# A two-layer hybrid trunk: three small moves in the order of VectorE, ScalarE and the load queue

## The chip, the cores and the metric

The kernel runs on one core of one Trainium2 chip. The metric is the device time of one execution in microseconds: 747.57 us before the change, the median of 3 runs (747.02 to 748.11).

## What is computed

256 tokens of width 1024 go through two layers in float32. Each layer has a token mixer and a gated ConvFFN, each behind an RMSNorm whose scale, shift and gate come from a conditioning vector c (adaLN). Layer 0 mixes by three dilated attention groups with 16 heads, layer 1 by gated linear attention (GLA) with 4 heads in chunks of 64 tokens.

```python
for i in range(2):
    mod = silu(c) @ w_ada[i] + b_ada[i]            # shift, scale, gate; twice
    h = rmsnorm(x, norm_mix[i]) * (1 + sc1) + sh1
    y = dilated_mixture(h, ...) if i == 0 else gla_mixer(h, ...)
    x = x + g1 * y
    h = rmsnorm(x, norm_ffn[i]) * (1 + sc2) + sh2
    x = x + g2 * conv_ffn(h, ...)
return rmsnorm(x, norm_final)

# gla_mixer, per head and chunk
gk = log_sigmoid(glr @ w_gate + b_gate) / 16
bcum = cumsum(gk);  blast = bcum at the chunk's end
q_t, k_t, k_d = q * exp(bcum), k * exp(-bcum), k * exp(blast - bcum)
A = tril(q_t @ k_t.T);  o = A @ v + q_t @ state
```

## The kernel before

**Weights.** Every product keeps float32 accuracy by splitting both factors into a high and a low part. A weight tile goes through four steps: SP's queue loads it into one of 4 `raw` buffers, ScalarE casts the high part `whi` (L236; L484 in the first pass), VectorE subtracts it for the low part `wlo` (L240; L582), and TensorE makes three products of each pair of blocks (L255 to L257): hi x hi, lo x hi, hi x lo. `whi` and `wlo` have 3 buffers each. SP's queue issues its loads in order, and a load waits there until its buffer is free.

**Order.** The order of instructions on each engine comes from a timeline simulation when the program is built; `behind(...)` is the only means by which the source bends it. It says that an instruction is to be placed behind another in that order and adds no wait by itself.

**The first pass (about 14 to 48 us)** computes q, k and v of head pairs 0 and 1, one k-tile (`kt` = 0 to 7) after another. For each kt, SP loads 2 x 512 KB of adaLN weights and a weight tile of 1920 columns (`load_w`, L589 to L595): 768 columns that the first 6 blocks need (`FRONT`) and 1152 more (`REST`). VectorE makes the dot products of the adaLN weights with c (L179), ScalarE turns each into the scale or shift (`mod`, L190 and L192) and makes `hhi` (L558), VectorE `hlo` (L574). TensorE's products of a front are L521.

**The pairs (about 50 to 262 us).** For pair u = 2 to 7 there are three groups g of queries and keys. Each has one weight tile `wqk` (1 MB). After each group's products `evacuate` takes q and k out of PSUM: for g = 0 in high and low parts (ScalarE L841, L842, VectorE `q` L845 twice and `k` L847), for g = 1 and 2 plainly (`k` L835). Ahead of group 2's products stand the 12 transposes (L798, `turn_all`) of the probabilities `pn` (VectorE L762, L763) of the pair before. At group 2, the first product takes its inputs from copies (`level`, shown as `q`) that share their buffer with a pair's q. Then come two tiles `wv` of 1536 columns for the values, whose subtractions are 128x768 twice each, then the scores and the softmax. Between them VectorE takes adaLN dot products of later sub-layers (`next_half`, 512 KB each, three spare buffers, loads at L691, dots at L179): three behind group 1 and three behind group 2.

**The gates (about 485 to 502 us).** `gates_of` (L1340) runs twice: for head 0, and for heads 1 to 3 together (tiles of 768 columns). It makes the decay sums `cs` by a scan (L1359), `u` = cs less its value at the chunk's end (L1362), and from these `e_q`, `e_k` and `e_d` by exponentials on ScalarE. `scaled_head` (L1449) multiplies q and k by them into `q_t`, `k_t`, `k_d`; `masked_head` makes the products L1475 of them. `head(n)` splits the q and k weights of head n, two subtractions of 128x1024.

Of the kernel before, what the change touches and what calls it, by code (L numbers as in the profile page):

```python
# [16 lines left out]
ALU = mybir.AluOpType  # L17

P = 128
# [9 lines left out]
CH = 64  # L29
# [30 lines left out]
def trunk(ctx: ExitStack, tc: tile.TileContext, I, out):  # L60
    nc = tc.nc
# [18 lines left out]
    @contextmanager  # L80
    def behind(*those):

        with ExitStack() as st:
            for i in those:
                st.enter_context(tc.issue_after(i.ins))
            yield
# [65 lines left out]
    for n in range(2):  # L152
        c = slice(512 * n, 512 * n + 512)
# [68 lines left out]

    last_load, copied, last_lo, dotted = [None], [None], [None], [None]

    def split(src, n, dmas=1, after=((), ()), late=(), low=(), view=None):
        raw = wraw.tile([P, 2048], F32, tag="raw", name="raw")
        for i in range(dmas):
            c = slice(n * i // dmas, n * (i + 1) // dmas)
            last_load[0] = nc.sync.dma_start(raw[:, c], src[:, c])
        hi = wspl.tile([P, 2048], F32R, tag="whi", name="whi")  # L230
        lo = wspl.tile([P, 2048], F32R, tag="wlo", name="wlo")
        part = view or (lambda w: w)
        for i in range(0, n, n // 2):
            c = slice(i, i + n // 2)
            with behind(*after[i > 0]):
                copied[0] = nc.scalar.copy(part(hi[:, c]), part(raw[:, c]))  # L236
        for i in range(0, n, n // 2):
            c = slice(i, i + n // 2)
            with behind(*(late if i else low)):
                last_lo[0] = nc.vector.tensor_tensor(part(lo[:, c]), part(raw[:, c]), part(hi[:, c].bitcast(F32)), op=ALU.subtract)  # L240
        return hi, lo
# [230 lines left out]
    part = tmp.tile([P, T], F32, tag="sqacc", name="part")  # L472
# [22 lines left out]
    for i, (g, n) in enumerate(ROWS):  # L495
        for first in range(0, n, P):
            c = slice(at, at + P)
# [90 lines left out]

    def load_w(kt, *queue):  # L589
        raw = wholes[1] if kt == 2 else wraw.tile([P, 2048], F32, tag="raw", name="raw")  # L590
        for c in (slice(0, 6 * P), slice(6 * P, 15 * P)) if kt < 3 else (slice(0, 15 * P),):
            with behind(*queue):
                last_load[0] = nc.sync.dma_start(raw[:, c], I["w0"][kt][:, c])
            queue = last_load[:1]
        return raw  # L595
# [27 lines left out]
    done = front(0, ((0, 0),), range(2 * NG), last_row)  # L623
    done = front_values(0, ((0, 0),), done)
    done = front(0, ((1, 0), (0, 1)), range(2 * NG), done)
    done = front_values(0, ((1, 0),), done)
    done = back_terms(0, HIGH, done)
    done = front_values(0, ((0, 1),), done)
# [261 lines left out]
    for u in range(NPAIR):  # L890
# [15 lines left out]
        if u < 2:  # L906
            for g in range(NG):
                evacuate(q, k, g, (pqk, pqk1)[u][2 * g], (pqk, pqk1)[u][2 * g + 1], *first_values[1:])
        else:
            for g in range(NG):  # L910
                low = negated[-1:] if (u, g) == (2, 2) else ()
                w = split(I["wqk"][u - 2, g], 2048, after=(ready, ready) if (u, g) == (2, 2) else ((), ()), low=low, late=low)
                if (u, g) == (2, 2):
                    with behind(last_lo[0]):
                        for _ in range(4):
                            second_pair[2]()
                    for _ in range(2):
                        next_half(norms[-1], turned[1], done)
                if (u, g) == (2, 1):
                    with tc.issue_after(last_load[0].ins):  # L920
                        bias = load_bias(1)
                    with behind(last_lo[0]):
                        for _ in range(4):
                            before[2]()
                    with behind(done):
                        second_pair = scores(1, *held, bias, *mm_k)
                pqk = bank("pqk", "p")
                pq, pk = pqk[:, :T], pqk[:, T:]
                for kt in range(KT):
                    s, e = kt == 0, kt == KT - 1  # L930


                    hk = early_level if u == 2 and g < 2 and kt == 0 else level if (u, g) > (3, 1) and g != 1 and kt == 0 else h[kt]
                    with behind(*(last_t if (g, kt) == (2, 0) else last_s if u == 2 and kt == 0 else [])):
                        mm3(pq[:, :T], parts(w, 2 * P * kt), hk, s, False)
                    mm_k = [mm3(pk[:, :T], parts(w, 2 * P * kt + P), hk, False, e)]
                if g == 1:
                    turn_all(before, pt := new_pt(), *mm_k)
                if (u, g) == (NPAIR - 1, 2):
                    copy_level((o_hi[OLEVEL], o_lo[OLEVEL]), *turned[-2:-1])  # L940
                done = evacuate(q, k, g, pq, pk)
                if (u, g) == (2, 2):
                    turn_all(second_pair, second_pt := new_pt(), *mm_k)
                if (u, g) == (2, 0):
                    first_loads.append(last_load[0])
                if g == 0:
                    ready = evacuated[:1]
                if u > 2:
                    for _ in range((0, 3, 3)[g]):
                        next_half(done)  # L950
                if g == 2 - (u > 2):
                    second = list(evacuated)
            if u == 4:
                with behind(last_load[0]):
                    nc.sync.dma_start(x_all, I["xT"])
        if u > 0:
            pv = [bank("pv", "p") for _ in range(2)]
            for half in range(2):
                with behind(*chain[7]):


                    if half == 1 and u < 4:
                        hi, lo = (first_values[:1], ()) if u == 1 else (second[:1], second[1:])
                    elif u == 2:
                        hi, lo = exps[7:8], last_dot[:1]
                    else:
                        hi = lo = ()
                    w = split(I["wv"][u - 1, half], 1536, after=(hi, hi if u < 3 else ()), low=lo, late=(*lo, done) if u == 2 and half == 0 else lo if u == 2 else ())
                    if u == 2 and half == 1:
                        for _ in range(3):  # L970
                            next_half(last_lo[0])
                if u > 1 and half == 0:
                    with tc.issue_after(last_load[0].ins):
                        bias = load_bias(u)
                for k4 in range(4):
                    kt = 4 * half + k4
                    wv = parts(w, 384 * k4, 384)
                    for t in range(2):
                        ht = [y[:, P * t : P * t + P] for y in h[kt]]
                        with behind(*(last_t if u == 2 and kt == 0 else [])):  # L980
                            last_pv[:] = [mm3(pv[t][:, :384], ht, wv, kt == 0, kt == KT - 1)]
# [358 lines left out]
    def gates_of(first, n):  # L1340
        def new(name, tag, columns=n * T):
            return gt([P, columns], name, tag=f"{tag}{min(first, 1)}")
# [12 lines left out]
        with behind(*offsets):  # L1355
# [2 lines left out]
        cs = new("cs", "cs")  # L1358
        nc.vector.tensor_tensor_scan(cs, keep[:, : n * T], sp, 0.0, op0=ALU.mult, op1=ALU.add)  # L1359
        cs4 = cs.rearrange("p (n t c) -> p n t c", t=2, c=P)  # L1360
        u = new("u", "C")
        offsets.append(nc.vector.tensor_tensor(u.rearrange("p (n t c) -> p n t c", t=2, c=P), cs4,  # L1362
                                               cs4[:, :, :, CH - 1 : CH].to_broadcast([P, n, 2, P]), op=ALU.subtract))
        e_d, e_q, e_k = (new(name, t) for name, t in (("e_d", "D"), ("e_q", "A"), ("e_k", "B")))
        d4 = e_d.rearrange("p (n t c) -> p n t c", t=2, c=P)
        nc.scalar.activation(e_k, u, AF.Exp, scale=1.0 / 16)
# [42 lines left out]
    with behind(last):  # L1409
        last = log_gates()  # L1410
    pv.append([bank("pv", "t") for _ in range(2)])
    gates = [gates_of(*part) for part in PARTS]
    with behind(*low_rank):
        w = columns(2, 0)
        next_ada(last_lo[0])
# [11 lines left out]
    def head(hd, **kw):  # L1427
        y = heads[hd]
        if hd == 0:
            y["w"] = split(I["w_qk_b"][0][:, KT * P :], KT * P)  # L1430
            y["pq"], y["pk"] = early_q, bank("pqk", "p")[:, :T]
        else:
            y["w"] = split(I["w_qk_b"][hd], 2048, **kw)
            pqk = bank("pqk", "p")
            y["pq"], y["pk"] = pqk[:, :T], pqk[:, T:]
# [103 lines left out]
    scaled_head(0)  # L1539
    head(1)  # L1540
    last = project_head(1, range(KT))
    head(2, low=first_kt[:1], late=first_kt[:1])
    last = masked_head(0, last)
    level = {kt: [gt([P, T], "lv", F32R, tag=tg) for tg in tags] for kt, tags in ((0, ("A0", "B0")), (1, ("C0", "D0")))}
    with behind(*copies):
# [156 lines left out]
```

## Time and profile before

| | before |
|---|---|
| median of 3 runs | 747.57 us (747.02 to 748.11) |
| profiled execution | 750.7 us, span 748.9 us |
| TensorE (PE) busy | 738.4 us, 99% |
| VectorE (DVE) busy | 645.5 us, 86% |
| ScalarE (ACT) busy | 490.0 us, 65% |
| DMA | 187.20 MB, mean 250 GB/s |

By stages, each busy time in us:

| window | TensorE | VectorE | ScalarE | DMA |
|---|---|---|---|---|
| 14 to 48 (first pass) | 33.21 | 32.37 | 24.71 | 412 GB/s |
| 100 to 246 (pairs 3 to 7) | 143.69 | 128.77 | 88.98 | 287 GB/s |
| 486 to 504 (gates) | 17.62 | 16.55 | 13.30 | 259 GB/s |

A row of a timeline gives: start in us, duration in us, engine and line, operation, output<-inputs, shapes, how many (x2 means two in a row in one line, whose duration runs from the first's start to the last's end), and in square brackets how long the engine had been idle and what ended that. Durations of matmuls are modelled and overlap: the row of 128x256 products has 0.28 us each, while they start 0.11 to 0.12 us apart. SPq rows are the issue of a DMA, not its transfer.

### The profile page before, as it was taken

The page shows a single profiled execution, that of the slowest core. Times are in us where ns is not written, and L with a number is a line of the kernel's source. Part 1 is how long each engine was busy: PE and PEld are TensorE (multiplying, and loading weights), DVE is VectorE, ACT ScalarE, POOL GpSimd, SP SyncE. Part 2 cuts the span into 40 slices and gives each one's busy share as a digit, 9 for nine tenths or more (in the row PEclk, how much of TensorE's full clock was granted, in tenths as well). Part 3 has the DMA queues.
Part 4 walks back from the last instruction along what each step waited for, and adds up shares of the span by engine and source line. Part 5 has one row for each costly group of instructions (what it writes and reads, how often), then busy time and mean ns, then how long its engine had stood idle before and what let it go on. Part 6 is the DMA issues. An engine that isn't in the chain of part 4 may idle for free.

```text
span 748.9 us, 16025 instructions
## 1 busy us (share of the span) xinstructions
PE 738.4 (99%) x6371; PEld 723.3 (97%) x6371; DVE 645.5 (86%) x1196; ACT 490.0 (65%) x967; POOL 30.8 (4%) x60
## 2 busy tenths in 40 slices
PE   9999999999999999999999999999999999999997
PEld 7999999999999999999999999999999999999996
DVE  6998998889988869999999886898969999997592
ACT  7686766556556568766766555866768676666551
POOL 1001010101101010000000100000010000000100
PEclk9999999999999999999999999999999999999999
DMA  9997779788788338877645997766758766774621
GB/s 340 412 399 272 261 267 393 251 274 312 251 302 281 114 140 305 307 262 263 226 161 190 322 327 242 282 232 225 274 184 284 279 221 233 206 182 159 206 97 57
DMA packets 40779, 187.20 MB, mean 250 GB/s; under 512 B 9170, under 2 KB 11866, under 8 KB 28032
## 3 DMA queue, kind: packets, MB, share of 16 engines
q1 hardware_dynamic: 40320, 185.73, 70.9%
q8 instruction: 50, 0.82, 0.4%
q10 hardware_dynamic: 304, 0.34, 0.1%
q14 instruction: 25, 0.20, 0.1%
q0 software_dynamic: 80, 0.11, 0.0%
HBM read 185.06 MB, written 1.10 MB: 249 GB/s over the span
## 4 chain that ended last, share of the span: by engine, by line
PE 85%; DMA 7%; DVE 5%; ACT 1%; issue 1%; DVEq 0%; SPq 0%; ACTq 0%
PE pab L256 11%; PE pab L255 11%; PE pab L257 10%; PE pd L255 5%; PE pd L257 5%; PE pd L256 5%; PE pqk L255 5%; PE pqk L257 4%; PE pqk L256 4%; DMA raw<-in_w 3%; PE pv L256 2%; PE pv L257 2%; PE pv L255 2%; PE py L255 2%; PE py L256 2%; PE py L257 2%
## 5 line engine op out<-in xcount | busy, mean ns | idle before, releaser
L240 DVE TENSOR_TENSOR wlo<-raw,whi 128x1024 fp32r<-128x1024 f32 (+5 forms) x248 | 264.5, 1094 | 25.8 <-ACT whi L236 25.0
L236 ACT CAST whi<-raw 128x1024 fp32r<-128x1024 f32 (+5 forms) x248 | 222.6, 943 | 96.4 <-PE pab L256 55.0
L256 PE MATMUL pab<-hlo,whi 128*128 128x256 f32 x672 | 184.9, 277 | 0.0
L257 PE MATMUL pab<-hhi,wlo 128*128 128x256 f32 x672 | 184.9, 276 | 0.0
L255 PE MATMUL pab<-hhi,whi 128*128 128x256 f32 x672 | 182.9, 277 | 0.0
L256 PEld LDWEIGHTS pab<-hlo,whi 128*128 128x128 f32 x672 | 126.1, 188 | 0.5 <-DVE hlo L335 0.4
L257 PEld LDWEIGHTS pab<-hhi,wlo 128*128 128x128 f32 x672 | 126.2, 188 | 0.0
L255 PEld LDWEIGHTS pab<-hhi,whi 128*128 128x128 f32 x672 | 125.0, 188 | 0.4 <-ACT hhi L333 0.3
L179 DVE CUSTOM_DVE_ANT_0 ada_raw<-ada_raw,c_bc 128x1024 f32<-128x1024 f32 x82 | 97.5, 1222 | 12.3 <-DMA ada_raw<-in_w_ada 12.1
L255 PE MATMUL pqk<-hhi,whi 128*128 128x256 f32 x354 | 97.7, 278 | 0.0
L256 PE MATMUL pqk<-hlo,whi 128*128 128x256 f32 x354 | 97.3, 277 | 0.0
L257 PE MATMUL pqk<-hhi,wlo 128*128 128x256 f32 x354 | 96.0, 277 | 0.2 <-DVE wlo L240 0.2
L257 PE MATMUL pd<-ghi,wlo 128*128 128x256 f32 x308 | 84.9, 276 | 0.0
L256 PE MATMUL pd<-glo,whi 128*128 128x256 f32 x308 | 84.9, 276 | 0.0
L255 PE MATMUL pd<-ghi,whi 128*128 128x256 f32 x308 | 84.7, 276 | 0.0
L255 PEld LDWEIGHTS pqk<-hhi,whi 128*128 128x128 f32 x354 | 66.5, 188 | 0.1
L256 PEld LDWEIGHTS pqk<-hlo,whi 128*128 128x128 f32 x354 | 66.5, 188 | 0.0
L257 PEld LDWEIGHTS pqk<-hhi,wlo 128*128 128x128 f32 x354 | 65.6, 188 | 0.4 <-DVE wlo L240 0.4
L256 PEld LDWEIGHTS pd<-glo,whi 128*128 128x128 f32 x308 | 57.8, 188 | 0.0
L257 PEld LDWEIGHTS pd<-ghi,wlo 128*128 128x128 f32 x308 | 57.8, 188 | 0.0
L255 PEld LDWEIGHTS pd<-ghi,whi 128*128 128x128 f32 x308 | 57.7, 188 | 0.0
L256 PE MATMUL pv<-wlo,hhi 128*128 128x384 f32 (+2 forms) x160 | 52.9, 332 | 0.0
(321 smaller groups left out, 1494.5 us busy)
## 6 DMA issues: line engine op xcount, KB each, us to landing
raw<-in_w_up SPq DMA_DIRECT2D x42, 1024.0 KB, 5.0
ada_raw<-in_w_ada SPq DMA_DIRECT2D x22, 1024.0 KB, 5.2
raw<-in_w_down SPq DMA_DIRECT2D x28, 704.0 KB, 4.4
ada_raw<-in_w_ada SPq DMA_DIRECT2D x38, 512.0 KB, 6.2
raw<-in_wqk SPq DMA_DIRECT2D x18, 1024.0 KB, 6.8
raw<-in_wv SPq DMA_DIRECT2D x14, 768.0 KB, 6.8
raw<-in_w SPq DMA_DIRECT2D x5, 960.0 KB, 12.8
raw<-in_w_v_b SPq DMA_DIRECT2D x6, 768.0 KB, 5.1
```

Source lines behind the costliest of these rows:

```text
L179: i = dotted[0] = nc.vector.tensor_tensor_reduce(w, w, c_bc, op0=ALU.mult, op1=ALU.add, scale=1.0, scalar=0.0, accum_out=dot,)
L236: copied[0] = nc.scalar.copy(part(hi[:, c]), part(raw[:, c]))
L240: last_lo[0] = nc.vector.tensor_tensor(part(lo[:, c]), part(raw[:, c]), part(hi[:, c].bitcast(F32)), op=ALU.subtract)
L255: mm(ps, a[0], b[0], start=start, stop=False)
L256: mm(ps, a[0], b[1], start=False, stop=False)
L257: return mm(ps, a[1], b[0], start=False, stop=stop)
```

## The change

It has three parts; the orders of TensorE and GpSimd stay as they were.

1. **Values' weights in the pairs.** In pairs 3 to 7 the two subtractions for the first `wv` tile are placed behind `keys_done`, the low part of group 0's key (`done` of g = 0, the instruction of L847).
2. **First pass.** `load_w` loads the tiles of kt = 3 and 4 in two transfers as well (768 and 1152 columns), as for kt = 1 and 2.
3. **Gates.** `gates_of` is cut in two; the second half, `factors_of`, makes `u` and the exponentials. For heads 1 to 3 it is called from within head 2's `split`, between its two subtractions, by the new argument `between`, and the second subtraction is placed behind `u`.

```diff
-    def split(src, n, dmas=1, after=((), ()), late=(), low=(), view=None):
+    def split(src, n, dmas=1, after=((), ()), late=(), low=(), view=None, between=None):
...
             c = slice(i, i + n // 2)
+            if i and between:
+                late = between()
             with behind(*(late if i else low)):
                 last_lo[0] = nc.vector.tensor_tensor(part(lo[:, c]), part(raw[:, c]), part(hi[:, c].bitcast(F32)), op=ALU.subtract)
...
-        for c in (slice(0, 6 * P), slice(6 * P, 15 * P)) if kt < 3 else (slice(0, 15 * P),):
+        for c in (slice(0, 6 * P), slice(6 * P, 15 * P)) if kt < 5 else (slice(0, 15 * P),):
...
                 if g == 0:
-                    ready = evacuated[:1]
+                    ready, keys_done = evacuated[:1], done
...
                     else:
-                        hi = lo = ()
-                    w = split(I["wv"][u - 1, half], 1536, after=(hi, hi if u < 3 else ()), low=lo, late=(*lo, done) if u == 2 and half == 0 else lo if u == 2 else ())
+                        hi, lo = (), (keys_done,) if u > 2 and half == 0 else ()
+                    late = lo if u == 2 or half == 0 else ()
+                    if (u, half) == (2, 0):
+                        late = *lo, done
+                    w = split(I["wv"][u - 1, half], 1536, after=(hi, hi if u < 3 else ()), low=lo, late=late)
...
         cs4 = cs.rearrange("p (n t c) -> p n t c", t=2, c=P)
+        return new, cs4, n
+
+    def factors_of(new, cs4, n, *after):
         u = new("u", "C")
-        offsets.append(nc.vector.tensor_tensor(u.rearrange("p (n t c) -> p n t c", t=2, c=P), cs4,
-                                               cs4[:, :, :, CH - 1 : CH].to_broadcast([P, n, 2, P]), op=ALU.subtract))
+        with behind(*after):
+            offsets.append(nc.vector.tensor_tensor(u.rearrange("p (n t c) -> p n t c", t=2, c=P), cs4,
+                                                   cs4[:, :, :, CH - 1 : CH].to_broadcast([P, n, 2, P]), op=ALU.subtract))
         e_d, e_q, e_k = (new(name, t) for name, t in (("e_d", "D"), ("e_q", "A"), ("e_k", "B")))
...
-    gates = [gates_of(*part) for part in PARTS]
+    gates = [factors_of(*gates_of(*PARTS[0]))]
+    sums_1 = gates_of(*PARTS[1])
...
-    head(2, low=first_kt[:1], late=first_kt[:1])
+    def later_factors():
+        gates.append(factors_of(*sums_1, *last_lo))
+        return offsets[-1:]
+
+    head(2, low=first_kt[:1], between=later_factors)
```

What this makes of the order, at three places. Line numbers of the changed kernel are higher by 2 to 10 than those before.

VectorE in a pair from 3 on, at the end of the softmax of the pair before and behind group 0's products. Before:

```order
L762 TENSOR_SCALAR pn<-prob,m 128x256
L763 TENSOR_SCALAR pn<-prob,m 128x128
L240 TENSOR_TENSOR wlo<-raw,whi 128x768 x2
L845 SCALAR_TENSOR_TENSOR q<-pqk,q 64x256 x2
L847 TENSOR_TENSOR k<-pqk,k 128x256
L240 TENSOR_TENSOR wlo<-raw,whi 128x768
L802 COPY pt<-t 128x512
L835 COPY k<-pqk 128x256
```

and now:

```order
L764 TENSOR_SCALAR pn<-prob,m 128x256
L765 TENSOR_SCALAR pn<-prob,m 128x128
L847 SCALAR_TENSOR_TENSOR q<-pqk,q 64x256 x2
L849 TENSOR_TENSOR k<-pqk,k 128x256
L242 TENSOR_TENSOR wlo<-raw,whi 128x768 x3
L804 COPY pt<-t 128x512
L837 COPY k<-pqk 128x256
```

The two subtractions went behind q and k, and stand directly ahead of the third.

ScalarE in the first pass, from the last cast of kt = 4 to the last of kt = 5. Before:

```order
L484 CAST whi<-raw 128x768
L190 ACTIVATE mod<-dot,one_b,small 128x1
L484 CAST whi<-raw 128x768
L192 ACTIVATE mod<-dot,small 128x1
L558 ACTIVATE hhi<-early_x,mod 128x256
L558 ACTIVATE xr<-early_x,mod 128x256
L484 CAST whi<-raw 128x384
```

and now:

```order
L486 CAST whi<-raw 128x768
L190 ACTIVATE mod<-dot,one_b,small 128x1
L192 ACTIVATE mod<-dot,small 128x1
L486 CAST whi<-raw 128x768
L560 ACTIVATE hhi<-early_x,mod 128x256
L560 ACTIVATE xr<-early_x,mod 128x256
L486 CAST whi<-raw 128x384
```

The cast of kt = 5's front went behind the second `mod`; at kt = 3, 4, 6 and 7 the order stays cast, then `mod`.

VectorE in the gates, from the scan for heads 1 to 3 on. Before:

```order
L1359 SCALAR_TENSOR_TENSOR cs<-keep,sp 128x768
L1362 TENSOR_TENSOR u<-cs 128x768
L1369 TENSOR_TENSOR e_d<-cs 128x3x128
L1459 TENSOR_TENSOR k_t<-pqk,e_k 128x256
L1463 SCALAR_TENSOR_TENSOR q_t<-early_q,e_q 128x256
L1465 TENSOR_TENSOR k_d<-pqk,e_d 128x128
L240 TENSOR_TENSOR wlo<-raw,whi 128x1024 x2
L1459 TENSOR_TENSOR k_t<-pqk,e_k 128x256
```

and now:

```order
L1364 SCALAR_TENSOR_TENSOR cs<-keep,sp 128x768
L1378 TENSOR_TENSOR e_d<-cs 128x3x128
L1469 TENSOR_TENSOR k_t<-pqk,e_k 128x256
L1473 SCALAR_TENSOR_TENSOR q_t<-early_q,e_q 128x256
L1475 TENSOR_TENSOR k_d<-pqk,e_d 128x128
L242 TENSOR_TENSOR wlo<-raw,whi 128x1024
L1371 TENSOR_TENSOR u<-cs 128x768
L242 TENSOR_TENSOR wlo<-raw,whi 128x1024
L1469 TENSOR_TENSOR k_t<-pqk,e_k 128x256
```

`u` went from ahead of everything of head 0 to between head 2's subtractions. On ScalarE the exponentials `e_k` and `e_q` of heads 1 to 3 went with it, behind the two casts of head 3's weights; and head 0's masked copy (L1478) now stands ahead of head 3's subtractions instead of behind them.

## The prediction

> **What bounds the kernel now.** I read the page's first part, then TensorE's and VectorE's waits in the stretch of the head pairs (100 to 246 us), then the timelines of the engines around each place that the diff touches.
>
> ```profile
> span 748.9 us, 16025 instructions
> PE 738.4 (99%) x6371; PEld 723.3 (97%) x6371; DVE 645.5 (86%) x1196; ACT 490.0 (65%) x967; POOL 30.8 (4%) x60
> ```
>
> TensorE is busy 99%: it is the bound taken over the whole, and only its few stops can be won back. The waits of the pairs' stretch (line waited for: us in total, times, longest), TensorE's and below them VectorE's:
>
> ```profile
> PE pqk L255 <- DVE k L847: 2.3, 3, 0.8
> ```
> ```profile
> DVE ada_raw L179 <- DMA ada_raw<-in_w_ada: 7.2, 7, 2.2
> ```
>
> TensorE stops three times for VectorE, 2.3 us. But VectorE itself stops seven times for a DMA. So inside the pairs two loops run beside each other, and a gain on TensorE lasts only if VectorE's loop can follow. That is the choice on which part A hangs.
>
> **A, the pairs.** The place, in pair 4, on TensorE, VectorE, ScalarE and the SP queue (the order of TensorE's and GpSimd's instructions is the same before and after):
>
> ```profile
> 140.01 1.47 PE L798 MATMUL t<-ident,pn 128*128 128x128 f32 x12
> 142.21 0.36 PE L255 MATMUL pqk<-q,whi 128*128 128x256 f32 x1 [0.73 <-DVE k L847]
> ```
> ```profile
> 138.92 1.82 DVE L240 TENSOR_TENSOR wlo<-raw,whi 128x768 fp32r<-128x768 f32 x2
> 140.77 0.86 DVE L845 SCALAR_TENSOR_TENSOR q<-pqk,q 64x256 fp32r<-64x256 f32 x2
> 141.64 0.42 DVE L847 TENSOR_TENSOR k<-pqk,k 128x256 fp32r<-128x256 f32 x1
> 141.98 0.95 DVE L240 TENSOR_TENSOR wlo<-raw,whi 128x768 fp32r<-128x768 f32 x1
> ```
> ```profile
> 138.80 0.77 ACT L841 ACTIVATE q<-pqk 64x256 fp32r<-64x256 f32 x2
> 139.59 0.37 ACT L842 CAST k<-pqk 128x256 fp32r<-128x256 f32 x1
> ```
> ```profile
> 139.01 2.09 SPq L229 DMA_DIRECT2D raw<-in_wqk  x2
> 144.43 0.33 SPq L229 DMA_DIRECT2D raw<-in_wv  x1
> 145.90 2.62 SPq L691 DMA_DIRECT2D ada_raw<-in_w_ada  x3
> ```
>
> Two subtractions L240 (1.82 us) stand between pn and q, k; the change puts them behind k. Then q waits for ScalarE instead: its halves end near 139.2 and 139.6, k's cast at 139.59 + 0.37 = 139.96. So VectorE's q runs at 139.2 and 139.65, k at about 140.1 to 140.5. The twelve transposes end by about 141.4, after k: the stop of 0.73 goes, and with it about 0.09 of restart (that first matmul takes 0.36 where its neighbours take 0.28). Over three pairs that is 2.3 + 3 x 0.09 = 2.6 us, the upper bound; at the level of k alone, 1.6 us more than now is the most that one pair could carry to the next.
>
> What pays: VectorE has waited for ScalarE a little, so its third L240 starts near 142.2 instead of 141.98, +0.2 in pairs where ScalarE is that late, and I take 0.3 over all five (in three of them the DMA stops take part of it up). And what is behind them on VectorE:
>
> ```profile
> 144.65 1.22 DVE L179 CUSTOM_DVE_ANT_0 ada_raw<-ada_raw,c_bc 128x1024 f32<-128x1024 f32 x1
> ...
> 153.81 1.23 DVE L179 CUSTOM_DVE_ANT_0 ada_raw<-ada_raw,c_bc 128x1024 f32<-128x1024 f32 x1 [2.16 <-DMA ada_raw<-in_w_ada]
> ```
>
> The row at 144.65 frees a buffer when it ends (145.87); at 145.90 SP issues the next three loads; at 153.81 VectorE has waited 2.16 us for them. From there VectorE works to the next pair's pn with no stop that TensorE causes. Since VectorE waits in this loop for the load and not for TensorE, an earlier TensorE doesn't shorten it: it is at best unchanged, by my estimate 0.3 us later. TensorE meets it again at the end of the pairs, at the first transpose of the last pair's pn, ahead of which the last piece of pn is written:
>
> ```profile
> 256.70 0.49 PE L784 MATMUL t<-ident,pn 128*128 128x128 f32 x3
> ```
> ```profile
> 255.65 0.28 DVE L763 TENSOR_SCALAR pn<-prob,m 128x128 f32<-128x128 f32 x1
> ```
>
> 256.70 - (255.65 + 0.28) = 0.77 us is all that TensorE may come earlier there. So A gives 0.77 - 0.3 = about 0.45 us, and the rest turns into new waits at the transposes (L798 of later pairs, L784). Each pair's moved pair of L240 also frees a raw buffer 1.6 us later, and the second load of the pair's wqk (the second of the x2 row at 139.01, which ran behind that release at 140.75) is issued that much later. The first wqk load is still under way then, so I cost it at nothing; if that cover is gone, it is the slow rival below. Bounds of A: -2.8 to +2.6.
>
> **B, the first pass.** The first weight cast and the mod row behind it on ScalarE for tiles 3 and 5, the same places on VectorE and on TensorE, and the DMA engines' answer for 6 to 36 us:
>
> ```profile
> 28.15 0.84 ACT L484 CAST whi<-raw 128x768 fp32r<-128x768 f32 x1 [1.86 <-DMA raw<-in_w]
> 28.90 0.29 ACT L192 ACTIVATE mod<-dot,small 128x1 f32<-128x1 f32 x1
> ...
> 38.23 0.84 ACT L484 CAST whi<-raw 128x768 fp32r<-128x768 f32 x1 [1.40 <-DMA raw<-in_w]
> 38.98 0.29 ACT L192 ACTIVATE mod<-dot,small 128x1 f32<-128x1 f32 x1
> ```
> ```profile
> 28.27 0.09 DVE L179 DVE_READ_ACCUMULATOR2_ANT dot<- 128x1 f32 x1
> 29.02 0.96 DVE L582 TENSOR_TENSOR wlo<-raw,whi 128x768 fp32r<-128x768 f32 x1 [0.67 <-ACT whi L484]
> ...
> 39.10 0.96 DVE L582 TENSOR_TENSOR wlo<-raw,whi 128x768 fp32r<-128x768 f32 x1 [0.27 <-ACT whi L484]
> ...
> 41.12 0.42 DVE L574 TENSOR_TENSOR hlo<-xr,hhi 128x256 fp32r<-128x256 f32 x1
> ```
> ```profile
> 29.87 0.96 PE L521 MATMUL pqk<-hhi,whi 128*128 128x256 f32 x6 [0.62 <-ACT hhi L558]
> ...
> 31.52 0.95 PE L521 MATMUL pqk<-hlo,whi 128*128 128x256 f32 x6
> ...
> 41.91 0.84 PE L521 MATMUL pqk<-hlo,whi 128*128 128x256 f32 x6
> ```
> ```profile
> DMA packets 3039, 12.16 MB, mean 405 GB/s; under 512 B 361, under 2 KB 363, under 8 KB 3037
> ```
>
> The second piece of a split tile, 128 x 1152 x 4 bytes = 0.59 MB, is 1.46 us at 405 GB/s, so the first lands that much earlier: tile 3's cast could start at 26.7. Its mod row must then wait for the dot that ends at 28.36; hhi and TensorE follow 0.5 us earlier than now, and VectorE's chain behind it 0.66 earlier. At tile 5, which isn't split, the change has mod ahead of the cast on ScalarE. The dot before it moves from 38.84 to about 38.4 (VectorE's earlier chain meets an adaLN load), so mod ends at 38.7, the cast starts at 38.75 instead of 38.23, and VectorE's 39.10 becomes 39.6. So does its hlo: 41.12 + 0.42 + 0.5 = 42.05, where TensorE used it at 41.91. The 0.5 won at tile 3 is waited away at tile 5, and 0.15 to 0.2 more. B: -0.2. Bounds: if VectorE is not earlier at all, the cast starts at 39.2 and B is -0.6; if tile 5 does no harm, the gain at the hlo row, +0.7. Two more issues on SP (0.33 us each in the rows of this queue) lie in a queue that runs 12 us ahead. The Trainium skill, "DMA: Bandwidth & Descriptors", section Bandwidth, speaks against B: it wants transfers of at least 1 MiB for 75% of peak and gives 341 GB/s at 1 MB. An estimate by that page: a tile's 0.98 MB at 341 instead of 405 GB/s is 0.45 us later, twice, and B would be -1.1. The trace disagrees: the 405 GB/s here is a stream of pieces of 0.4 to 1 MB.
>
> **C, the gates.** TensorE and VectorE around the first masked head:
>
> ```profile
> 493.38 0.28 PE L257 MATMUL pqk<-hhi,wlo 128*128 128x256 f32 x1
> 493.88 0.49 PE L1475 MATMUL a<-q_t,k_t 128*128 128x128 f32 x2 [0.23 <-DVE q_t L1463]
> ...
> 495.22 0.39 PE L257 MATMUL pqk<-hhi,wlo 128*128 128x256 f32 x1 [0.16 <-DVE wlo L240]
> ```
> ```profile
> 491.74 0.96 DVE L1362 TENSOR_TENSOR u<-cs 128x768 f32<-128x768 f32 x1
> 492.61 0.55 DVE L1369 TENSOR_TENSOR e_d<-cs 128x384 f32<-128x384 f32 x1
> 493.08 0.42 DVE L1459 TENSOR_TENSOR k_t<-pqk,e_k 128x256 f32<-128x256 f32 x1
> 493.41 0.42 DVE L1463 SCALAR_TENSOR_TENSOR q_t<-early_q,e_q 128x256 f32<-128x256 f32 x1
> 493.75 0.28 DVE L1465 TENSOR_TENSOR k_d<-pqk,e_d 128x128 f32<-128x128 f32 x1
> 493.95 2.35 DVE L240 TENSOR_TENSOR wlo<-raw,whi 128x1024 fp32r<-128x1024 f32 x2
> ```
>
> u (0.87 us from its start to e_d's) leaves the place ahead of e_d, so q_t ends at 492.96 instead of 493.83 and the first wlo half at about 494.3 instead of 495.15. TensorE reaches the masked head at 493.5: the first stop, 0.50 between starts less a pace of 0.11, 0.39 us, goes. It then wants the wlo near 494.5: the second stop, 0.34 between the same kind of starts, and its 0.11 of restart go too. Sum 0.84; I take 0.8. Late next: u ends at 495.1 between the two halves, the second half at 496.2 for products that come near 497; ScalarE's e_k and e_q for the other heads move behind head 3's casts to 495.1 to 496.8, so q_t of head 1 is 0.3 us later, for a masked head on TensorE at 500.5. Bounds: 0.4 (only the first stop) to 0.84.
>
> **Sum.** 0.45 - 0.2 + 0.8 = 1.05 us. The profiled execution took 750.7 us (span 748.9 and 1.8 around it), 3.1 above the runs' median; it would become 749.65. On the median: 747.57 - 1.05 = 746.5 us.
>
> **Rivals.** *All stops of TensorE count* (17 in 100): A is 2.6, so 2.6 - 0.2 + 0.8 = 3.2 and 744.4 us. For it speak the 99% and that the wait is on TensorE's own row; against it the 2.16 at 153.81, which shows VectorE held by a load, not by TensorE. The Trainium skill, "Perfetto Trace Analysis", section Identifying the Most-Contended Engine, is on this rival's side: it takes the engine of highest occupancy, TensorE by its weight loads (97% here), as the one to be served first. The rows agree on which engine that is; whether it keeps the gain no run here shows yet.
>
> *A hole in the DMA stream* (13 in 100, the slower side): each pair's second wqk load, issued 1.6 us later, finds the first one done or nearly done, and all that is queued behind it (wv, then the three adaLN loads) lands up to 0.9 us later. VectorE's stops at the L179 rows then grow by 0.9 in each of four pairs, 3.6 in all, of which the 0.77 of slack takes some: A is -2.8, the sum -2.2, the time 749.8. It decides from about 0.45 us a pair on. For it: the SP row of 139.01 and the waits of 7.2 us; against it: the first wqk load is 1 MB, 2.6 us at 405 GB/s, so something is still in flight.
>
> *The loop gives nothing* (20 in 100): VectorE's lateness in the pairs is 0.2 in each of four, 0.8, and eats A's slack; A is 0 and B -0.6 at worst; 747.57 - 0.8 + 0.2 to 0.6 = 747.0 to 747.4. B would then not do what it says.
>
> **How the numbers follow.** The forecast has 50 in 100, its own range 745.5 to 747.2. Two runs of this kernel can be told apart from about 0.2%, 1.5 us: faster is below 746.07, slower above 749.07. Faster: the first rival's 17 and two fifths of the forecast, 37. Slower: nearly all of the DMA hole, 12. The rest, 51, is within. The range goes from 744.0, which takes in the first rival, to 748.6, which leaves out most of the hole.
>
> **What would show it.** In pairs 4, 5 and 7 the first product of group 2 right behind its transposes, with no wait on k; but new waits of TensorE at L798's or L784's successors for pn, with the L179 waits for a DMA as long as before (+0 to 0.3). If those waits grow by 0.5 or more a pair, the hole is right; if no new wait on pn appears and the pairs end 2 us earlier, the first rival. In the first pass the stop at 29.87 halves, and a new one for hlo stands near 42. At 493 to 495 no stop over 0.1 us. I am wrong by most if VectorE's loop is moved by something that I cost at nothing: the order in which SP's loads land.

## The result, and the profile after

The changed kernel takes 753.26 us (median of 4 runs, 752.82 to 753.66) against 747.47 us before (4 runs, 747.02 to 748.11): slower, ratio 1.0077, 95% interval 1.0059 to 1.0094. The forecast was 746.5 us with a range from 744.0 to 748.6: a gain was forecast, and the change is a loss of 5.8 us. The profiled execution of the change took 753.66 us (span 751.9), as long as the others. The profiled execution before had taken 750.7, which is 3 us more than the others of its kernel; that difference turns out to matter.

The page of the changed kernel, its first lines:

```profile
span 751.9 us, 16029 instructions
PE 739.8 (98%) x6371; PEld 723.3 (96%) x6371; DVE 646.2 (86%) x1196; ACT 489.7 (65%) x967; POOL 29.6 (4%) x60
```

TensorE and VectorE are busy nearly as long as before (738.4 and 645.5 us), so most of the loss went into waits. Those of VectorE between 100 and 262 us and of TensorE between 100 and 265 us, in the changed kernel (line waited for: us in total, times, longest; line numbers are 2 higher in the pairs):

```profile
DVE ada_raw L179 <- DMA ada_raw<-in_w_ada: 8.9, 7, 2.4
DVE m L761 <- ACT prob L772: 5.5, 5, 1.3
DVE q L847 <- ACT k L844: 5.2, 5, 1.2
DVE wlo L242 <- ACT whi L236: 1.3, 5, 0.4
```
```profile
PE pv L257 <- DVE k L837: 1.8, 4, 0.8
PE py L258 <- DVE o L825: 1.6, 1, 1.6
PE pqk L257 <- DVE k L849: 1.1, 2, 0.7
```

Three things are new. VectorE waits about 1.0 us in each pair ahead of q, for ScalarE's cast of k. It waits longer for the adaLN loads (7.2 us in the profile that the prediction read). And TensorE waits where it didn't: for k of group 2, whose copy frees the bank that the values' second half needs, and 1.6 us at the start of layer 0's output projection, behind the last pair's outputs. Of the 2.3 us for k of group 0, which A was to remove, 1.1 us are left.

Pair 5 in the changed kernel, on VectorE, then ScalarE, the SP queue and TensorE:

```profile
170.29 0.28 DVE L765 TENSOR_SCALAR pn<-prob,m 128x128 f32<-128x128 f32 x1
171.55 0.86 DVE L847 SCALAR_TENSOR_TENSOR q<-pqk,q 64x256 fp32r<-64x256 f32 x2 [0.98 <-ACT k L844]
172.42 0.42 DVE L849 TENSOR_TENSOR k<-pqk,k 128x256 fp32r<-128x256 f32 x1
172.76 2.89 DVE L242 TENSOR_TENSOR wlo<-raw,whi 128x768 fp32r<-128x768 f32 x3
...
177.37 1.21 DVE L179 CUSTOM_DVE_ANT_0 ada_raw<-ada_raw,c_bc 128x1024 f32<-128x1024 f32 x1
...
183.41 0.42 DVE L837 COPY k<-pqk 128x256 f32<-128x256 f32 x1
184.98 1.23 DVE L179 CUSTOM_DVE_ANT_0 ada_raw<-ada_raw,c_bc 128x1024 f32<-128x1024 f32 x1 [1.15 <-DMA ada_raw<-in_w_ada]
```
```profile
168.89 1.55 ACT L236 CAST whi<-raw 128x768 fp32r<-128x768 f32 x2
170.35 0.76 ACT L843 ACTIVATE q<-pqk 64x256 fp32r<-64x256 f32 x2
171.14 0.38 ACT L844 CAST k<-pqk 128x256 fp32r<-128x256 f32 x1
```
```profile
170.65 4.54 SPq L229 DMA_DIRECT2D raw<-in_wqk  x2
```
```profile
183.88 0.44 PE L257 MATMUL pv<-whi,hhi 128*128 128x384 f32 x1 [0.83 <-DVE k L837]
```

q starts as ScalarE's k cast ends (171.14 + 0.38 = 171.52), although in the source q uses only ScalarE's q. It is so in all five pairs: by the list of waits above q waited five times for k's cast, and VectorE's own k (L849), which uses that cast, never. So the wait for k's cast was taken at q, two places early; why it stands there isn't shown. The three subtractions then end at 175.65 (172.76 + 2.89), k of group 2 is 0.8 us too late for TensorE, and the second of the two loads in the SP row is issued only when a buffer comes free: the row is 4.54 us long, where that of the same pair had been 1.43 before (169.94) and that of pair 4 2.09.

At the places of the two other parts the trace looks as forecast. TensorE at tile 5 of the first pass and at the first masked head, in the changed kernel:

```profile
42.29 0.98 PE L523 MATMUL pqk<-hlo,whi 128*128 128x256 f32 x6 [0.32 <-DVE hlo L576]
```
```profile
497.38 0.28 PE L259 MATMUL pqk<-hhi,wlo 128*128 128x256 f32 x1
497.49 0.38 PE L1485 MATMUL a<-q_t,k_t 128*128 128x128 f32 x2
```

The new stop for hlo is there, and the masked head follows 0.11 us behind the product before it, without a stop.

### The profile page after: what moved, and what is told of

It is laid out like the page before. It is cut to its first block, busy times and chain, and to the rows that moved or that the text cites. A ratio compares the mean times of both kernels' runs of the same rounds, so it can differ in the third digit from the quotient of the medians.

```text
span 751.9 us, 16029 instructions
## 1 busy us (share of the span) xinstructions
PE 739.8 (98%) x6371; PEld 723.3 (96%) x6371; DVE 646.2 (86%) x1196; ACT 489.7 (65%) x967; POOL 29.6 (4%) x60
## 4 chain that ended last, share of the span: by engine, by line
PE 84%; DVE 8%; DMA 5%; ACT 2%; issue 1%; SPq 0%; DVEq 0%; ACTq 0%
PE pab L258 10%; PE pab L259 10%; PE pab L257 10%; PE pd L257 5%; PE pd L259 5%; PE pd L258 5%; PE pqk L257 5%; PE pqk L258 4%; PE pqk L259 4%; DVE wlo L242 3%; PE pv L257 3%; PE pv L258 3%; PE pv L259 2%; DVE ada_raw L179 2%; PE py L258 2%; PE py L257 2%
## 5 line engine op out<-in xcount | busy, mean ns | idle before, releaser
L179 DVE CUSTOM_DVE_ANT_0 ada_raw<-ada_raw,c_bc 128x1024 f32<-128x1024 f32 x82 | 97.4, 1218 | 13.2 <-DMA ada_raw<-in_w_ada 12.8
L257 PE MATMUL pv<-whi,hhi 128*128 128x384 f32 (+2 forms) x160 | 52.5, 337 | 1.8 <-DVE k L837 1.8
```

What stands on the lines that cost most here:

```text
L179: i = dotted[0] = nc.vector.tensor_tensor_reduce(w, w, c_bc, op0=ALU.mult, op1=ALU.add, scale=1.0, scalar=0.0, accum_out=dot,)
L257: mm(ps, a[0], b[0], start=start, stop=False)
```

## The experiments

Two theories stood when the first four experiments were set up. Theory 1: A loses because VectorE stands idle for 1.0 us a pair ahead of q. Theory 2: A loses because the raw buffer comes free later, so that the second wqk load and all loads behind it are late. The times are medians of 4 to 11 runs; the waits and rows come from one profiled execution of each kernel. Of each diff the deciding lines are shown; `...` stands for lines that only carry `keys_done` and `late` along.

A number of the form "pn to first dots" below is read from VectorE's rows as in pair 5 above: the end of the last pn row (170.29 + 0.28 = 170.57) to the first L179 row (177.37) is 6.80 us.

**B and C without A.** Against the change, the pairs' placement is as before:

```diff
-                        hi, lo = (), (keys_done,) if u > 2 and half == 0 else ()
+                        hi = lo = ()
...
```

> Parts B and C without A: the pairs' two value subtractions stand ahead of group 0's q and k again. Both theories put the whole loss into the pairs, so both expect this near the kernel before: C takes 0.5 to 0.8 us off, B adds 0.4 to 0.6 (the wait for hlo at tile 5), 747.0 to 747.6 us. If it comes out above 749, the loss isn't in the pairs and both theories fall.

Measured: 746.96 us beside 747.48 of the kernel before, ratio 0.9999, interval 0.9989 to 1.0008. Without A there is no loss.

**A alone.**

```diff
-                        hi = lo = ()
+                        hi, lo = (), (keys_done,) if u > 2 and half == 0 else ()
...
```

> Part A alone. Both theories: all of the loss, 753 to 754 us, with VectorE idle about 1.0 us ahead of q in each of five pairs, TensorE's stops at the second bank of the values (for k of group 2) and one of 1.5 us at the start of the output projection. Below 750: A needs B or C for its loss.

Measured: 753.78 us, ratio 1.0091, interval 1.0077 to 1.0106. VectorE's waits between 100 and 262 us:

```profile
DVE ada_raw L179 <- DMA ada_raw<-in_w_ada: 9.8, 9, 2.7
DVE q L845 <- ACT k L842: 5.2, 5, 1.2
```

A costs 6.3 us. The whole change costs 5.8, which by the two intervals is no difference. TensorE stops for k of group 2 (2.0 us) and at the output projection (1.3 us), as expected, and 2.0 us more in two stops for k of group 0.

**Half of A.** One subtraction stays between pn and q, the second goes behind k:

```diff
-                        hi, lo = (), (keys_done,) if u > 2 and half == 0 else ()
-                    late = lo if u == 2 or half == 0 else ()
+                        hi, lo = (), ()
+                    late = lo if u == 2 else (keys_done,) if u > 2 and half == 0 else ()
...
```

> A by half: only the second of the two value subtractions goes behind group 0's k, the first stays between pn and q. Theory 1 (A loses because VectorE stands idle for 1.0 us a pair until ScalarE has cast k): the first subtraction, 0.9 us, fills just that time, VectorE does the same work without the idle time, and k is 0.9 us earlier than before: 745.5 to 747.5 us, idle ahead of q 0 to 0.2 us. Theory 2 (A loses because the raw buffer is freed later, so that the second wqk load and all loads behind it are late): the buffer is still freed about 1.35 us later than before, against 3.3 in the change, so about two fifths of the loss stays: 749.5 to 750.5 us.

Measured: 747.54 us, ratio 1.0002, interval 0.9993 to 1.0011. Pair 5 on VectorE, here and then in the kernel before:

```profile
166.66 0.28 DVE L763 TENSOR_SCALAR pn<-prob,m 128x128 f32<-128x128 f32 x1
166.85 0.95 DVE L240 TENSOR_TENSOR wlo<-raw,whi 128x768 fp32r<-128x768 f32 x1
167.93 0.86 DVE L845 SCALAR_TENSOR_TENSOR q<-pqk,q 64x256 fp32r<-64x256 f32 x2
168.80 0.42 DVE L847 TENSOR_TENSOR k<-pqk,k 128x256 fp32r<-128x256 f32 x1
169.14 0.95 DVE L240 TENSOR_TENSOR wlo<-raw,whi 128x768 fp32r<-128x768 f32 x1
```
```profile
168.99 0.28 DVE L763 TENSOR_SCALAR pn<-prob,m 128x128 f32<-128x128 f32 x1
...
171.91 0.42 DVE L847 TENSOR_TENSOR k<-pqk,k 128x256 fp32r<-128x256 f32 x1
```

The subtraction fills the time in which ScalarE casts k, and the loss is gone, as theory 1 had it; theory 2 had 749.5 to 750.5. But k 0.8 us sooner behind pn (169.22 - 166.94 = 2.3 us, before 172.33 - 169.27 = 3.1) brought nothing either.

**Keys first on both engines.** A whole, and ScalarE's two value casts behind its q and k:

```diff
-                        hi, lo = (), (keys_done,) if u > 2 and half == 0 else ()
+                        hi, lo = (ready, (keys_done,)) if u > 2 and half == 0 else ((), ())
...
-                    w = split(I["wv"][u - 1, half], 1536, after=(hi, hi if u < 3 else ()), low=lo, late=late)
+                    w = split(I["wv"][u - 1, half], 1536, after=(hi, hi if u < 3 or half == 0 else ()), low=lo, late=late)
...
```

> A whole, and ScalarE's two value casts moved behind its q and k of group 0 as well, so that k is cast 1.55 us sooner. Theory 1: VectorE finds k cast when pn is done, its idle time ahead of q falls from 1.0 to below 0.1 us, and the time to 745.5 to 747.5 us, unless the casts, now later, hold up the subtractions. Theory 2: the buffer is freed at least 1.3 us later than before, 749.5 to 752 us.

Measured: 747.89 us, ratio 1.0008, interval 1.0000 to 1.0017. That is 0.4 us above theory 1's range and 1.6 below theory 2's. VectorE in pair 5, and its waits for loads between 100 and 262 us:

```profile
169.08 0.44 DVE L763 TENSOR_SCALAR pn<-prob,m 128x128 f32<-128x128 f32 x1
169.54 0.86 DVE L845 SCALAR_TENSOR_TENSOR q<-pqk,q 64x256 fp32r<-64x256 f32 x2
```
```profile
DVE ada_raw L179 <- DMA ada_raw<-in_w_ada: 7.6, 6, 3.0
```

q starts 0.02 us behind pn, and nearly all of the loss is gone, as theory 1 had it. But the waits for adaLN loads, 7.6 us, are nearly those of the change (8.9) and cost next to nothing; TensorE's stops in this stretch are 1.0 us in all.

**A filler in the order before.** To see whether VectorE's lateness alone does it, an operation without effect was put behind k in pairs 3 to 7 of the kernel before:

```diff
                 if g == 0:
                     ready = evacuated[:1]
+                    if u > 2:
+                        with behind(done):
+                            nc.vector.tensor_tensor(c_bc[:, 0:768], c_bc[:, 0:768], c_bc[:, 0:768], op=ALU.max)
```

> The order of the kernel before, with one idle-like VectorE operation of 128x768 (an in-place maximum on c's copy, about 0.95 us, without effect on any value) behind k of group 0 in pairs 3 to 7. The raw buffer is freed as early as before, q and k are as early as before; only what follows on VectorE is 0.95 us later in each pair. Theory 1 (VectorE's loop has about 0.5 to 1 us a pair to spare, and A used up more): most of A's loss comes back, 751 to 753.5 us, with TensorE's stops for k of group 2 and VectorE's waits for adaLN loads at 7 to 10 us. Theory 2 (the late free buffer and the loads behind it): 747.5 to 748.5 us, since nothing on the queue is freed later than before ahead of the first dots.

Measured: 747.76 us, ratio 1.0006, interval 0.9997 to 1.0015. This is theory 2's number, and theory 1 falls in its simple form, that VectorE's lateness alone costs. But theory 2 had missed half of A by 2 us, where the buffer came free late. VectorE in pair 5 (L950 is the filler), and its waits for loads between 100 and 262 us:

```profile
167.75 0.28 DVE L763 TENSOR_SCALAR pn<-prob,m 128x128 f32<-128x128 f32 x1
...
169.79 0.86 DVE L845 SCALAR_TENSOR_TENSOR q<-pqk,q 64x256 fp32r<-64x256 f32 x2
170.66 0.42 DVE L847 TENSOR_TENSOR k<-pqk,k 128x256 fp32r<-128x256 f32 x1
171.00 1.19 DVE L950 TENSOR_TENSOR c_bc<-c_bc 128x768 f32<-128x768 f32 x1
172.12 0.95 DVE L240 TENSOR_TENSOR wlo<-raw,whi 128x768 fp32r<-128x768 f32 x1
...
174.79 1.21 DVE L179 CUSTOM_DVE_ANT_0 ada_raw<-ada_raw,c_bc 128x1024 f32<-128x1024 f32 x1
```
```profile
DVE ada_raw L179 <- DMA ada_raw<-in_w_ada: 2.4, 4, 1.1
```

The first dots come 6.76 us behind pn (174.79 - 168.03), as late as in the change (6.80), and yet TensorE doesn't wait in this stretch. The loads are quick here: 2.4 us of waits for them in place of 8.9.

**C alone.** The diff of part 3 and nothing else.

> Part C alone. By the prediction's term 0.8 us less: 746.7 us, with no stop of TensorE above 0.1 us at the first masked head and at the first low part of head 2. The rival, that something behind the gates takes it back: 747.5 us with the two stops gone and a new one later.

Measured: 746.69 us beside 747.49, ratio 0.9989, interval 0.9980 to 0.9998. The 0.8 us of the prediction is all there, and TensorE has no wait between 480 and 510 us, where it had two of 0.2 before. This is the one version whose gain can be told from nothing, and only just.

**B alone.** `kt < 5` in `load_w` and nothing else.

> Part B alone. By the prediction's term 0.2 us more: 747.7 us, the stop at tile 3 (0.8 with its restart) down to about 0.1 to 0.4 and a new one of 0.4 to 0.6 for hlo at tile 5. If tile 5 does no harm: 746.8 us.

Measured: 747.61 us, ratio 1.0003, interval 0.9994 to 1.0012. TensorE at tiles 3 and 5:

```profile
29.42 0.97 PE L521 MATMUL pqk<-hhi,whi 128*128 128x256 f32 x6
30.22 0.84 PE L521 MATMUL pqk<-hhi,wlo 128*128 128x256 f32 x6
31.22 0.95 PE L521 MATMUL pqk<-hlo,whi 128*128 128x256 f32 x6 [0.16 <-DVE hlo L574]
```
```profile
42.20 0.97 PE L521 MATMUL pqk<-hlo,whi 128*128 128x256 f32 x6 [0.29 <-DVE hlo L574]
```

Won at 29.4 (before: 29.87), given back at 42.2 (before: 41.91). The median is the one forecast, but a change of this size can't be told from nothing.

**The kernel before, a second profile.** No edit.

> A second profile of the unchanged kernel, since its first one took 3 us more than its median. If TensorE's stops for k in pairs 4, 5 and 7 (2.3 us) belong to the order of the instructions, as the prediction took it, they are there again, and the execution is about 750 us. If they belong to that one execution, in which the adaLN loads were late, there are none or one of them, VectorE's wait for adaLN loads is 2 to 4 us instead of 7.2, and the execution takes 746.5 to 748.5 us.

Measured: 748.01 us. Waits of VectorE for adaLN loads between 100 and 262 us, and TensorE's only wait between 100 and 265 us:

```profile
DVE ada_raw L179 <- DMA ada_raw<-in_w_ada: 5.5, 8, 1.1
```
```profile
PE pqk L255 <- DVE k L847: 0.2, 1, 0.2
```

The 2.3 us of stops that A was to remove weren't there. The time and the stops came out as expected for stops that belong to one execution; the waits for loads did not (2 to 4 us expected). The profiles of B and C without A, of B alone and of C alone, whose pairs have the order before, show no wait of TensorE at all in that stretch. That of the last experiment below, with the same order in the pairs, has one such stop for k of group 0 (and 0.3 us at the output projection):

```profile
PE pqk L257 <- DVE k L849: 0.9, 1, 0.9
```

Its profiled execution took 748.35 us against a median of 746.53, with 5.8 us of waits for adaLN loads. So these stops come with single executions: of six profiled executions with this order in the pairs, three have none.

**Both lags by other means.** Theory 3, formed from the filler and keys first: A loses where two lags meet. The dots are late, and the wqk load ahead of their loads is late too, because the buffer is freed later. Keys first frees the buffer late but has its dots early; the filler has its dots late but frees the buffer early. This kernel has both (the edits of keys first and of the filler):

> Keys first on both engines, which cost nothing, plus the 0.95 us of VectorE work behind k in pairs 3 to 7, which cost nothing either. Together they give VectorE's loop both lags of the change by other means: the raw buffer is freed some 4.2 us behind pn (before 1.7) and the first dots start some 6.7 us behind pn (before 5.3 to 6.2). Theory 3 (A loses because the two meet: the dots are late and the loads that they release stand behind a wqk load that is late too): most of A's 6.3 us comes back, 750.5 to 754 us, and VectorE's waits for adaLN loads are 7 to 10 us. If each lag is harmless for its own reason and they only add: 748 to 748.5 us. If what costs in A is only that VectorE waits idle for ScalarE: 747.5 to 748.5 us, since it waits for nothing here.

Measured: 751.18 us beside 747.21, ratio 1.0056, interval 1.0040 to 1.0071. Two edits that cost 0.4 and 0.3 us alone by their medians cost 4.0 us together. Pair 5 on VectorE, and its waits for the loads between 100 and 262 us:

```profile
169.69 0.86 DVE L845 SCALAR_TENSOR_TENSOR q<-pqk,q 64x256 fp32r<-64x256 f32 x2
170.56 0.42 DVE L847 TENSOR_TENSOR k<-pqk,k 128x256 fp32r<-128x256 f32 x1
170.91 0.95 DVE L950 TENSOR_TENSOR c_bc<-c_bc 128x768 f32<-128x768 f32 x1
171.77 2.69 DVE L240 TENSOR_TENSOR wlo<-raw,whi 128x768 fp32r<-128x768 f32 x3
```
```profile
DVE ada_raw L179 <- DMA ada_raw<-in_w_ada: 7.1, 8, 1.8
```

No wait for ScalarE ahead of q, and still nearly two thirds of A's loss. The means over pairs 4 to 6, from VectorE's rows as above (buffer free: end of the second 128x768 subtraction; second dots: first L179 row behind k of group 2; period: pn to the next pair's pn), with each kernel's median:

| kernel | pn to buffer free | pn to first dots | first to second dots | period | median |
|---|---|---|---|---|---|
| before, first profile | 1.7 | 5.8 | 8.5 | 29.9 | 747.5 |
| before, second profile | 1.7 | 5.9 | 7.7 | 29.4 | 747.5 |
| B and C without A | 1.7 | 6.4 | 7.1 | 29.3 | 747.0 |
| half of A | 3.2 | 6.3 | 6.9 | 28.9 | 747.5 |
| filler | 1.7 | 6.7 | 6.8 | 29.2 | 747.8 |
| keys first | 3.1 | 5.8 | 8.0 | 29.7 | 747.9 |
| keys first and filler | 3.9 | 6.5 | 7.6 | 30.2 | 751.2 |
| the change | 4.2 | 6.8 | 8.3 | 30.9 | 753.3 |
| A alone | 4.2 | 6.8 | 8.5 | 31.3 | 753.8 |

Each row is one profiled execution, and the first two show how far two of one kernel lie apart. In the three kernels of the table without a wait of TensorE in this stretch (B and C without A, half of A, filler) a pair takes 28.9 to 29.3 us on the mean. The period less "pn to first dots" and "first to second dots" is 15.6 to 16.1 us in every row: VectorE's loop is as long as the dots and the loads behind them make it. In the three slow kernels both are long, and TensorE pays in each pair.

That the two lags don't add is shown by the times. That they meet through the late wqk load is theory 3's account and not shown: in the first profile of the kernel before the loads took as long as in A alone, with the buffer free at 1.7, and half of A has the buffer free at 3.2, the dots at 6.3 and no loss. Keys first also moves two of ScalarE's casts, so this experiment doesn't test the late buffer by itself.

**Splitting more tiles.** C alone, and `kt < 7` in `load_w`:

> C, and the first pass's tiles 3 to 6 in two transfers instead of 3 and 4. The exchange of cast and mod on ScalarE then stands at tile 7, the first one that isn't split. If the first pass's length is set by when its last tile arrives, nothing is won over C alone: 746.5 to 747.0 us. If the stops at tiles 3 and 5 were the whole cost: 746.0 to 746.3 us.

Measured: 746.53 us beside 747.21, ratio 0.9995, interval 0.9986 to 1.0004. At tile 3 TensorE comes earlier by 0.4 us than in C alone (31.19 against 31.61 for the hlo row), but at 56 us, behind the pass, a new stop stands in this profile:

```profile
56.29 0.44 PE L257 MATMUL pv<-whi,hhi 128*128 128x384 f32 x1 [0.57 <-ACT v L869]
```

What was won in the first pass can't be told from nothing at the end.

## Why the prediction was wrong

The term that failed is A: 0.45 us of gain was forecast, with bounds of -2.8 to +2.6, and A alone costs 6.3 us.

**The base of A's gain** failed first. The prediction read 2.3 us of stops for k in pairs 4, 5 and 7 and took 0.45 us of gain from them. The second profile has 0.2 us of them. The warning stood in the prediction's own sum: the profiled execution was 3.1 us above the median, and this was carried along as a constant. Most of the 3.1 us was the stops themselves (2.3, and 0.3 of restarts by the prediction's own count), in an execution whose adaLN loads were late (7.2 us of waits, against 5.5 in the second profile and 2.1 in that of B and C without A). Without these stops the order before has next to nothing that A could win, and half of A, which brings k forward with hardly any idle time (0.4 us in all), gains nothing.

**"VectorE's q runs at 139.2 and 139.65"** was wrong by 0.8 us. That is 0.2 behind pn (139.00); in pair 4 of the changed kernel q started at 140.39, 1.0 behind pn (139.39), behind ScalarE's k cast. Before, 1.8 us of subtractions had covered that wait, so the trace couldn't show that q's wait reaches to the cast of k. VectorE's third subtraction started 4.2 us behind pn in place of 3.0: a lag of 1.2 us a pair, not 0.2. Of it 1.0 is the idle time, and 0.2 is the second subtraction, which takes 1.16 us there in place of 0.95.

**"I cost it at nothing"**, for the second wqk load, mis-sized the second lag. Its buffer came free 4.2 us behind pn in place of 1.7, not 1.6 but 2.5 us later, since the idle time counts too. The SP queue's own waits for a subtraction between 100 and 262 us grew from 16.1 to 31.4 us. The rival of a hole in the DMA stream had the right place, but gave 749.8 us. It priced the late loads alone, and these alone cost little: keys first, with 7.6 us of waits for them, costs 0.4. With VectorE late at the same time the cost is 4.0, by the experiment with both. The range was built from costs that add up, and these two don't. The prediction's sign for this rival, waits for adaLN loads that grow by 0.5 us a pair, doesn't decide: they grew by 0.3 a pair against the profile that it read (7.2 to 8.9) and by 0.7 against the second one (5.5).

**The slack of 0.77 us and the waits for pn.** The prediction looked for TensorE's next stops at the transposes. They came at the values' second bank, for k of group 2 (1.8 us), at the output projection (1.6 us) and still for k of group 0 (1.1 us); none was for pn. The late loop shows where VectorE frees a bank, not only where it writes an input.

**B's mechanism was right**, with the gain at tile 3 and the stop at tile 5 at the places named. 0.2 us of loss was forecast and 0.1 measured by the medians, which can't be told from nothing. Splitting cost no bandwidth that could be measured: the interval of B alone ends at 0.9 us of loss. The Trainium skill, "DMA: Bandwidth & Descriptors", section Bandwidth, asks for at least 1 MiB per transfer, and by the prediction's estimate from that page B would have lost 1.1 us; this queue doesn't bear that out.

**C was right**: 0.8 forecast, 0.8 measured (0.1 to 1.5 by the interval), and both stops are gone.

**The rival that all stops count** fell too: only one of six profiled executions has the 2.3 us of stops that it counted. The rival that the loop gives nothing was nearer, since there was next to nothing to win, but its 747.4 us at most has no loss in it either. What held TensorE in the changed kernel was VectorE's loop, at 86% busy. The Trainium skill, "Perfetto Trace Analysis", section Identifying the Most-Contended Engine, points at TensorE, and rightly by the busy share of its weight loads (96%).

What stays open: why the same loads, issued in the same order, land in 5.5 us in one execution and in 8.1 in another; whether the late wqk load is what makes the two lags cost more than their sum; and the 2 us between keys first with the filler and the change, for which the table has a first dot 0.3 us later and loads 0.7 us slower per pair, but no experiment of its own.

## What to carry to other kernels

Compare the profiled execution's time with the median before reading a stop as something to win: a stop that only the one profiled execution has is no gain, and a second profile of the same kernel shows it. When an operation moves ahead on its engine, ask for all that its wait, and those of the instructions right behind it, will now meet uncovered, and which buffer the operations that it passed were freeing. Two lags that are nearly harmless one by one can be costly together (0.4 and 0.3 us alone, 4.0 together here), so test them together.

## What the runs showed of the hardware

An adaLN load of 512 KB, issued behind the first dots of pair 4 at nearly the same moment with the same loads ahead of it, took 5.5 us from issue to landing in one kernel (half of A, issued at 145.72) and 8.1 us in another (keys first, 145.69), while the mean rate of both between 100 and 262 us is 269 GB/s. With these loads under way the rate between 148 and 150 us was 286 GB/s in the first and 167 in the second.

VectorE's in-place maximum of 128x768 took 1.19 us in pair 5 of the filler and 0.95 in the same pair of keys first with the filler, for the same operation. In the first GpSimd's casts of k (whose times are rough) ended within it, at 171.39; in the second they ended 0.04 us behind its start. In the changed kernel they end within the second value subtraction in all five pairs, and it takes 1.15 or 1.16 us each time. Why isn't shown.
